# Recurrent states moved as 2 KB rows and turned by products with the identity, in a decoder layer on one Trainium2 core

## The chip, the cores and the metric

The kernel runs on one core of a Trainium2 chip. The core has a matrix engine (TensorE, PE in the profile; its weight loads are listed apart as PEld), a vector engine (DVE), a scalar engine (ACT), a general engine (GpSimd, POOL) and a queue engine (SyncE, SP) that here only issues transfers. Each engine works through its own instructions in program order and waits on semaphores. Sixteen DMA engines move the data between device memory and the on-chip memory (128 partitions). Products are written to PSUM, of which a bank holds 128 x 512 numbers. The metric is the device time of the whole program in microseconds (us), lower being better.

## What is computed

One layer of a decoder for 256 prompt tokens and for 8 sample sequences with 4 new tokens each. A layer has an input projection, an RWKV-7 group of 16 heads, a sparse attention group of 16 heads, an output projection and a mixer of experts. The change touches the RWKV group of the samples alone. Each sample has, for each head, a state S of 64 x 64 (value x key), which is read, carried over four steps and written back:

```python
def step(S, inp):
    r_t, d_t, k_t, v_t, kk_t, a_t = inp
    sk = jnp.einsum('bhvk,bhk->bhv', S, kk_t)
    S = (S * d_t[:, :, None, :] - sk[..., None] * (kk_t * a_t)[:, :, None, :]
         + v_t[..., None] * k_t[:, :, None, :])
    return S, jnp.einsum('bhvk,bhk->bhv', S, r_t)
```

For 8 samples and 16 heads that is 2 MB of states in and 2 MB out. In device memory a state's rows are its 64 values v, each with 64 keys k (256 bytes).

## The kernel before

The program runs in stages, one after the other, each with several streams of work woven together: input projections with the prompt's recurrence, then the sample attention, then the prompt attention with the output projection, then the mixer. The order within a stage is written by generators: `weave` always advances the stream that is furthest behind by its weight. A scheduler, which runs a timeline of its own when the program is built, then sets the order on every engine, so a change in one stream moves rows of the others on all engines.

The stage of interest weaves three streams: `late` (the attention of the samples), `sample_states` followed by `sample_steps` (their recurrence), and `outcomes` (the end of the prompt's recurrence). It runs from about 556 to 756 us.

The attention stream has 20 units. For each, POOL gathers selected rows or SP loads window rows into tiles `co` (L453, L899; 512 KB each, a ring of 14), PE turns the keys (L920), multiplies with the queries (L939, new keys L945), ACT and DVE do the softmax, PE turns the probabilities (L964, L968) and applies them (L983). A `co` tile is given back when L983 has read it, and the gather of a later unit waits for that. L535 to L575 are the compressed branch and L1007 turns a finished output. The next stage uses the memory of these tiles again for its first loads (L1667 onward: prompt rows, gate weights, output weights).

The recurrence stream:

- `sample_states` loads four states at a time into the tile `big` (`S0`), one buffer, with 4 transfers a sample (L1240). Eight samples make 32 transfers. For each sample PE turns the 16 heads with 4 transposes of 128 x 128 (L1244) and ACT copies the bank to `S0T` (L1245): key on the partition, two heads side by side in the halves of the partitions.
- `sample_steps` begins with the first products of all eight samples, 128 products of 64 x 64 by 8 columns (L1259) into one bank, then 16 small copies to `Ua` and `Ya` (L1265, L1266).
- The coefficients between the four tokens (L1284 to L1287), the four steps (L1295, L1296), and the new states (L1322 on POOL, L1324 on PE, L1326 and L1327 on DVE) follow.
- For each sample PE turns the new state back with 4 transposes (L1332), ACT copies it to `S1` (L1334, two buffers), and SP writes it with 4 transfers (L1337).
- At the end come the group norm of `Ya` (L1342 to L1350) and the sum into `BV` (L1353, L1356).

All banks of this stream have the tag `ss`, of which there are two. In the profile a digit at the end of a name is left out, so `S1` stands there as `S`, `x1` as `x`.

Of the kernel before, what the change touches and what calls it, by code (L numbers as in the profile page):

```python
# [18 lines left out]
P = 128  # L19
# [129 lines left out]
def hybrid_decode_step(ctx: ExitStack, tc: tile.TileContext, a, outs, dbg=None):  # L149
    nc = tc.nc  # L150
    ve, sc, pe, gp, sy = nc.vector, nc.scalar, nc.tensor, nc.gpsimd, nc.sync
    stop = dbg.get("stop", 99) if dbg is not None else 99
# [34 lines left out]
    def bank(tag="pb"):  # L187
        places = [(pool, nm, n) for _, div in psum for t_, pool, nm, n in div for _ in range(n) if t_ == tag]
        turn[tag] = k = (turn.get(tag, -1) + 1) % len(places)
        pool, nm, n = places[k]  # L190
        return pool.tile([P, 512], F32, name=tag, tag=nm, bufs=n)
# [60 lines left out]
    ident = C0("ident")  # L252
# [108 lines left out]
    for q in range(8):  # L361
        pb = bank(("p0", "p1")[q % 2])
        for t in range(2):
            for e in range(2):
                k = 2 * q + e
# [32 lines left out]
    hs = (slice(0, 64), slice(64, 128))  # L398
# [820 lines left out]
            yield from outcome(s, 1, "ss", sp([P, 8, 64], "Y2", bufs=2, tag="PR"))  # L1219


    S0T = sPQ = sD = sBC = sUV = None

    def sample_states(sp):

        nonlocal S0T, sPQ, sD, sBC, sUV
        S0T, sS = sp([P, 8, 8, 64], "S0T"), sp([P, 8, 232], "sS")
        sPQ = sS[:, :, 0:64].rearrange("p j (q t) -> p q j t", q=2)
        sD = sS[:, :, 64:104]
        sBC = sS[:, :, 104:168].rearrange("p j (y t) -> p j y t", y=2)  # L1230
        sUV = sS[:, :, 168:232].rearrange("p j (y t) -> p j y t", y=2)
        sy.dma_start(sS[:, :, :200], RS[:, :, :])
        srw = a["state_rwkv"][0].rearrange("b (j2 jp h) v k -> b jp h v j2 k", jp=2, h=2)
        for b in range(8):
            if b % 4 == 0:
                S0 = sp([P, 4, 4, P], "big", bufs=1)
                for b_ in range(4):
                    for jp in range(2):
                        for h in range(2):
                            sy.dma_start(S0[hs[jp], b_, :, 64 * h:64 * h + 64], srw[b + b_, jp, h])  # L1240
                yield 4 if b else 6
            pb = bank("ss")
            for j2 in range(4):
                pe.transpose(pb[:, 128 * j2:128 * j2 + 128], S0[:, b % 4, j2, :], ident)  # L1244
            sc.copy(S0T[:, b].rearrange("p j v -> p (j v)"), pb)  # L1245
            yield 0.5

    def sample_steps(sm):
        nrw = outs[10][0].rearrange("b (j2 jp h) v k -> b jp h v j2 k", jp=2, h=2)
        Ua, Ya, Vc = sm([P, 4, 8, 8], "Ua"), sm([P, 4, 8, 8], "Ya"), sm([P, 4, 8, 8], "Vc")  # L1250
        b_ = bank("ss")
        bk = [b_[:, :256], b_[:, 256:]]
        for ph in range(2):
            for jj in range(4):
                for b in range(8):
                    for h in range(2):
                        q = (ph + h) % 2
                        j = 4 * q + jj
                        pe.matmul(bk[q][hs[h], 64 * jj + 8 * b:64 * jj + 8 * b + 8], S0T[hs[h], b, j, :],  # L1259
                                  sPQ[hs[h], :, j, b::8], start=True, stop=True)  # L1260
                yield 1
        for q in range(2):
            v5 = bk[q][:, :256].rearrange("p (j b q t) -> p q t j b", j=4, b=8, q=2)
            for t in range(4):
                ve.tensor_copy(Ua[:, t, 4 * q:4 * q + 4, :], v5[:, 0, t])  # L1265
                sc.copy(Ya[:, t, 4 * q:4 * q + 4, :], v5[:, 1, t])  # L1266
        gp.tensor_copy(Vc.rearrange("p t j b -> p j t b"), sUV[:, :, 0, :].rearrange("p j (t b) -> p j t b", t=4))
        yield 1

# [11 lines left out]
        for q in range(4):  # L1281
# [3 lines left out]
            pb = bank("ss")  # L1285
# [25 lines left out]
        for src, dst in ((sUV, UVt), (sBC, BCt)):  # L1311
            for q in range(2):
                pb = bank("ss")
# [4 lines left out]
        for j in range(8):  # L1318
            pb = bank("ss")
# [8 lines left out]
            yield 2  # L1328
        for b in range(8):
            pb = bank("ss")  # L1330
            for j2 in range(4):
                pe.transpose(pb[:, 128 * j2:128 * j2 + 128], S0T[:, b, 2 * j2:2 * j2 + 2, :].rearrange("p a b -> p (a b)"), ident)  # L1332
            S1 = sm([P, 4, P], "S1", bufs=2, tag="S0")
            sc.copy(S1.rearrange("p j c -> p (j c)"), pb)  # L1334
            for jp in range(2):
                for h in range(2):
                    sy.dma_start(nrw[b, jp, h], S1[hs[jp], :, 64 * h:64 * h + 64])  # L1337
            yield 0.5

        Yf = Ya.rearrange("p t j b -> p (t j b)")  # L1340
        pb = bank("ss")
# [4 lines left out]
        pb = bank("ss")  # L1346
# [281 lines left out]
    sp = Pool("sp", "left")  # L1628
# [129 lines left out]
    for t in range(2):  # L1758
        for q in range(4):
            x_ = x1c(t, 512 * q, 512)  # L1760
            normed = ve.tensor_scalar(x_, x_, lrr[:, t:t + 1], lv[:, t:t + 1], op0=OP.mult, op1=OP.add)
            pb = bank("pa")
            for e in range(4):
                pe.transpose(pb[:, 128 * e:128 * e + 128], x1c(t, 512 * q + 128 * e, 128), ident)
            for e in range(4):
                k = 4 * q + e
# [35 lines left out]
    rp([P, UG], "rows", bufs=NRW)  # L1802
    S1 = dp([P, 8, 2 * P], "S1")
    dp([P, NDB, P], "ur", bufs=NUR)
# [4 lines left out]
    got, rows_, last_dot = [0, 0], {}, []  # L1809
# [36 lines left out]
    for h in range(9):  # L1846
        S, QP = [], {2 * h - 2 + c: q_ for c, q_ in enumerate(QN)} if h else {}
        QN = [kq([P, NPR], "QP", bufs=6) for c in range(2)]
        for c in (2 * h, 2 * h + 1):
            if c < 16:  # L1850
                pb = bank("pj")
# [7 lines left out]
        if h in (3, 8):  # L1859
            with tc.issue_after(wl_[12 if h < 8 else -1]):  # L1860
                t = h // 8
# [188 lines left out]
    pb = bank("pb")  # L2050
# [39 lines left out]
    for k in range(P):  # L2090
# [12 lines left out]
        for t in range(2):  # L2103
            for wi, xi in ((ah, vh), (ah, vl), (al, vh)):
                for q in range(3):
                    n_ = min(512, FD - 512 * q)
                    pe.matmul(acc[3 * t + q][:, :n_], wi[:, P * t:P * t + P], xi[:, 512 * q:512 * q + n_],  # L2107
                              start=(k == 0 and wi is ah and xi is vh), stop=(k == P - 1 and wi is al))
# [7 lines left out]
        if 66 <= k < 114 and k % 6 == 0:  # L2116
            with tc.issue_after(ld_.ins):
# [6 lines left out]
                else:  # L2124
                    t_, nm = ((g2_, "ln2_g"), (b2_, "ln2_b"))[n_ // 2 - 2]
# [67 lines left out]
```

## Time and profile before

| what | value |
|---|---|
| runs, median (lowest to highest of 3) | 2453.99 us (2433.44 to 2458.53) |
| the profiled execution, its own time | 2450.29 us |
| its span, first to last instruction | 2448.5 us |
| mean granted clock of PE | 0.951 |
| state loads L1240: transfers, KB each | 32, 64 |
| state writes L1337: transfers, KB each | 32, 64 |

In the rows of the profile a group is line, engine, operation and `output<-inputs`, with the count behind an x. In a timeline a row stands for a run of equal instructions: start and length in us, and in brackets the idle time of the engine ahead of it with what ended it. The length includes the end of the last instruction, which overlaps the next row's start. The granted clock is the share of full speed that PE's clock had in that window.

### The profile page before, as it was taken

The page shows a single profiled execution, that of the slowest core. Times are in us where ns is not written, and L with a number is a line of the kernel's source. Part 1 is how long each engine was busy: PE and PEld are TensorE (multiplying, and loading weights), DVE is VectorE, ACT ScalarE, POOL GpSimd, SP SyncE. Part 2 cuts the span into 40 slices and gives each one's busy share as a digit, 9 for nine tenths or more (in the row PEclk, how much of TensorE's full clock was granted, in tenths as well). Part 3 has the DMA queues.
Part 4 walks back from the last instruction along what each step waited for, and adds up shares of the span by engine and source line. Part 5 has one row for each costly group of instructions (what it writes and reads, how often), then busy time and mean ns, then how long its engine had stood idle before and what let it go on. Part 6 is the DMA issues. An engine that isn't in the chain of part 4 may idle for free.

```text
span 2448.5 us, 42558 instructions
## 1 busy us (share of the span) xinstructions
PE 2255.8 (92%) x15628; PEld 1888.4 (77%) x15628; DVE 1762.0 (72%) x4049; ACT 823.4 (34%) x1601; POOL 1332.6 (54%) x1347
## 2 busy tenths in 40 slices
PE   7988999897988998679999999999999899999996
PEld 7877889894645565558888888887777788887885
DVE  4788766555563355687877777556777899998888
ACT  4433222223432334221111111111777544444343
POOL 5687522324355011666766556565443688886772
PEclk9989999998896799789999999999999999999998
DMA  7777885448578784979999999999664799999994
GB/s 219 215 232 233 257 236 172 131 135 250 200 248 250 249 274 172 317 253 348 317 367 377 391 371 387 345 395 345 186 188 142 284 362 360 358 367 356 345 360 183
DMA packets 327600, 684.07 MB, mean 279 GB/s; under 512 B 82270, under 2 KB 200992, under 8 KB 326464
## 3 DMA queue, kind: packets, MB, share of 16 engines
q1 hardware_dynamic: 246176, 342.58, 42.2%
q0 software_dynamic: 81216, 338.78, 38.6%
q8 instruction: 123, 2.02, 0.3%
q14 instruction: 85, 0.70, 0.1%
HBM read 665.69 MB, written 23.88 MB: 282 GB/s over the span
## 4 chain that ended last, share of the span: by engine, by line
PE 29%; DMA 9%; DVE 8%; issue 7%; POOL 4%; ACT 1%; POOLq 0%; DVEq 0%; SPq 0%; ACTq 0%
PE pb L2107 20%; DMA rows<-in_peer_u_g,gi 8%; POOL rows L453 4%; PE px L1945 3%; DVE rows L1825 2%; PE pa L1978 2%; PE pj L1855 2%; PE pt L1937 1%; PE fs L1997 1%; DVE sr L1586 1%; DVE vl L2100 1%; DMA wraw<-in_peer_wq 0%; ACT vh L2099 0%; PE pa L1690 0%; DVE cw L1586 0%
## 5 line engine op out<-in xcount | busy, mean ns | idle before, releaser
L1899 PE MATMUL ph<-Xfd,ur 128*128 128x256 f32 x2304 | 497.6, 379 | 0.0
L1899 PEld LDWEIGHTS ph<-Xfd,ur 128*128 128x128 f32 x2304 | 437.6, 190 | 59.4
L453 POOL DMA_INDIRECT rq<-in_peer_v_g,gi x256 | 382.2, 1493 | 145.8 <-DVE fP L2080 85.6
L453 POOL DMA_INDIRECT rows<-in_peer_u_g,gi x256 | 313.3, 1224 | 189.3 <-DVE rows L1825 119.0
L1825 DVE SCALAR_TENSOR_TENSOR rows<-rows,x1a 128x896 f32<-128x896 f32 x256 | 278.8, 1097 | 136.2 <-DMA rows<-in_peer_u_g,gi 135.5
L422 PE MATMUL pj<-XH,wl 128*128 128x288 f32 (+1 forms) x752 | 233.5, 311 | 15.8 <-DVE wl L417 9.1
L422 PE MATMUL pj<-XH,wh 128*128 128x288 f32 (+1 forms) x752 | 232.1, 309 | 14.6 <-DVE ss L752 6.0
L422 PE MATMUL pj<-XL,wh 128*128 128x288 f32 (+1 forms) x752 | 228.0, 303 | 0.0
L2080 DVE SCALAR_TENSOR_TENSOR fP<-rq,ge,fP 128x640 f32<-128x640 f32 x254 | 223.7, 881 | 2.5
L2107 PE MATMUL pb<-vl,ah 128*128 128x512 f32 (+1 forms) x768 | 205.9, 376 | 0.8
L2107 PE MATMUL pb<-vh,al 128*128 128x512 f32 (+1 forms) x768 | 205.0, 375 | 0.0
L1900 ACT COPY AW<-ph 128x256 f32<-128x256 f32 x128 | 76.6, 612 | 370.5 <-PE ph L1899 362.7
L2107 PE MATMUL pb<-vh,ah 128*128 128x512 f32 (+1 forms) x768 | 185.6, 376 | 13.4 <-ACT vh L2099 10.9
L415 ACT CAST wh<-wraw 128x512 fp32r<-128x512 f32 (+1 forms) x188 | 115.1, 616 | 240.3 <-PE pj L422 191.1
L2107 PEld LDWEIGHTS pb<-vh,ah 128*128 128x128 f32 x768 | 144.1, 194 | 35.5 <-ACT vh L2099 13.9
L422 PEld LDWEIGHTS pj<-XH,wl 128*128 128x128 f32 (+1 forms) x752 | 145.8, 194 | 26.8 <-DVE wl L417 12.4
L476 DVE SCALAR_TENSOR_TENSOR CA<-co,wbc,CA 128x256 f32<-128x256 f32 x248 | 131.5, 568 | 46.5 <-DMA co<-in_cache_cmp_kv,gidx 46.5
L422 PEld LDWEIGHTS pj<-XH,wh 128*128 128x128 f32 (+1 forms) x752 | 146.1, 194 | 21.0 <-ACT wh L415 6.7
L2107 PEld LDWEIGHTS pb<-vl,ah 128*128 128x128 f32 x768 | 144.1, 194 | 22.7 <-DVE vl L2100 3.8
L2107 PEld LDWEIGHTS pb<-vh,al 128*128 128x128 f32 x768 | 144.5, 194 | 19.3
L422 PEld LDWEIGHTS pj<-XL,wh 128*128 128x128 f32 (+1 forms) x752 | 146.4, 195 | 1.5 <-issue 1.2
L417 DVE TENSOR_TENSOR wl<-wraw,wh 128x512 fp32r<-128x512 f32 (+1 forms) x141 | 100.8, 722 | 49.0 <-ACT wh L415 48.7
(871 smaller groups left out, 4335.6 us busy)
## 6 DMA issues: line engine op xcount, KB each, us to landing
ur<-in_peer_u_t SPq DMA_DIRECT2D x128, 576.0 KB
wraw<-in_w_in SPq DMA_DIRECT2D x152, 256.0 KB
cw<-in_w_out SPq DMA_DIRECT2D x32, 512.0 KB
wraw<-in_w_out SPq DMA_DIRECT2D x32, 512.0 KB
wraw<-in_peer_wq SPq DMA_DIRECT2D x32, 512.0 KB
cw<-in_peer_wq SPq DMA_DIRECT2D x32, 512.0 KB
wraw<-in_w_in SPq DMA_DIRECT2D x64, 128.0 KB
co<-in_state_win_kv SPq DMA_DIRECT2D x16, 512.0 KB
```

Source lines behind the costliest of these rows:

```text
L415: sc.copy(wh[:, :, :n], w[:, :, :n])
L417: i_ = en.tensor_tensor(wl[:, :, :n], w[:, :, :n], wh[:, :, :n].bitcast(F32), OP.subtract)
L422: last[2] = pe.matmul(pb[:n, :nt], wi[:, k, :n], xi[(o + k) // 8][:, (o + k) % 8, :nt], start=(o + k == 0 and wi is wh and xi is xh), stop ...
L453: gp.indirect_dma_start(out=dst, out_offset=None, in_=rows_, in_offset=bass.IndirectOffsetOnAxis(ap=ix, axis=0))
L476: ve.scalar_tensor_tensor(d_, x_, w_, d_, op0=OP.mult, op1=OP.add)
L1825: i_ = ve.scalar_tensor_tensor(r_, r_, 1.0, X1a[t], op0=OP.mult, op1=OP.mult, accum_out=h_)
L1855: pe.matmul(pb[:, :NPR], w[:, k, :], XT[:, o + k, :], start=(o + k == 0), stop=(o + k == 15))
L1899: mm = pe.matmul(ph[:, :NPR], w[:, e, :], Xfd[:, e, :], start=(e == 0), stop=(e == NDB - 1))
L1900: return mm, sc.copy(AW[:, i1 // 64, :, i1 % 64], ph[:, :NPR])
L1945: pin(pe.matmul(px[:, 128 * e:128 * e + 128].rearrange("p (c j) -> p c j", c=2), oT[:, e, :], AW[:, :, 4 * u + e, :], start=True, stop=True))
L2080: ve.scalar_tensor_tensor(fP[t], r_, w_, fP[t], op0=OP.mult, op1=OP.add)
L2107: pe.matmul(acc[3 * t + q][:, :n_], wi[:, P * t:P * t + P], xi[:, 512 * q:512 * q + n_], start=(k == 0 and wi is ah and xi is vh), stop=(k ...
```

## The change

Of a head's 64 rows eight follow one another on a partition now: partition 8j + o of a half holds rows 8o to 8o + 7 of head 2j + h, 512 numbers in one piece, 2 KB in device memory. A sample takes 2 transfers (one for each h) where it took 4. Since the rows of a head no longer lie on 64 partitions, the state is turned in 8 steps i, each for both halves, by a product of the 64 x 64 slice with the identity: 16 products a sample where 4 transposes were. The copy to `S0T` puts the columns back in the order of v. On the way out the same is done in reverse, with the products reading every eighth column of `S0T`. The first products of a sample (L1255 now) follow its turn, in a bank of their own, with one DVE and one ACT copy of 128 x 32; `Ua` and `Ya` are made in `sample_states`. From L1264 to L1323 line numbers are 3 lower than before, from L1340 on 2 lower.

```diff
+    def state_rows(st_, b, h):
+        return bass.AP(tensor=st_.tensor, offset=st_.offset + 65536 * b + 4096 * h, ap=[[8192, 8], [512, 8], [1, 512]])
...
-                S0 = sp([P, 4, 4, P], "big", bufs=1)
+                S0 = sp([P, 4, 8, 64], "big", bufs=1)
                 for b_ in range(4):
-                    for jp in range(2):
-                        for h in range(2):
-                            sy.dma_start(S0[hs[jp], b_, :, 64 * h:64 * h + 64], srw[b + b_, jp, h])
+                    for h in range(2):
+                        sy.dma_start(S0[hs[h], b_].rearrange("p i k -> p (i k)"), state_rows(a["state_rwkv"][0], b + b_, h))
...
-            for j2 in range(4):
-                pe.transpose(pb[:, 128 * j2:128 * j2 + 128], S0[:, b % 4, j2, :], ident)
-            sc.copy(S0T[:, b].rearrange("p j v -> p (j v)"), pb)
+            for i in range(8):
+                for h in range(2):
+                    pe.matmul(pb[hs[h], 64 * i:64 * i + 64], S0[hs[h], b % 4, i, :], ident[hs[h], hs[h]], start=True, stop=True)
+            sc.copy(S0T[:, b].rearrange("p j (o i) -> p j o i", i=8), pb.rearrange("p (i j o) -> p j o i", i=8, j=8))
             yield 0.5
+            pb = bank("ss")
+            for ph in range(2):
+                for jj in range(4):
+                    for h in range(2):
+                        j = 4 * ((ph + h) % 2) + jj
+                        pe.matmul(pb[hs[h], 8 * j:8 * j + 8], S0T[hs[h], b, j, :], sPQ[hs[h], :, j, b::8],
+                                  start=True, stop=True)
+            v4 = pb[:, :64].rearrange("p (j q t) -> p q t j", j=8, q=2)
+            ve.tensor_copy(UY[0][:, :, :, b], v4[:, 0])
+            sc.copy(UY[1][:, :, :, b], v4[:, 1])
+            yield 1
...
-            for j2 in range(4):
-                pe.transpose(pb[:, 128 * j2:128 * j2 + 128], S0T[:, b, 2 * j2:2 * j2 + 2, :].rearrange("p a b -> p (a b)"), ident)
-            S1 = sm([P, 4, P], "S1", bufs=2, tag="S0")
-            sc.copy(S1.rearrange("p j c -> p (j c)"), pb)
-            for jp in range(2):
+            rows_ = S0T[:, b].rearrange("p j (o i) -> p i (j o)", i=8)
+            for i in range(8):
                 for h in range(2):
-                    sy.dma_start(nrw[b, jp, h], S1[hs[jp], :, 64 * h:64 * h + 64])
+                    pe.matmul(pb[hs[h], 64 * i:64 * i + 64], rows_[hs[h], i], ident[hs[h], hs[h]], start=True, stop=True)
+            S1 = sm([P, 512], "S1", bufs=2, tag="S0")
+            sc.copy(S1, pb)
+            for h in range(2):
+                sy.dma_start(state_rows(outs[10][0], b, h), S1[hs[h]])
```

The removed block of first products in `sample_steps` (L1249 to L1266) is the same work with all samples in one bank.

How this moves the rows of PE at the fourth and fifth state, that is at the seam between the two loads of four. `CT` holds the identity. Before, from the fourth state's transposes to the fifth's:

```order
L1244 MATMUL ss<-CT_61,big 128x128 x4
L1209 MATMUL ss<-CT_61,YT_106 128x128 x4
L552 MATMUL sa<-im,CT_141 128x32
...
L939 MATMUL sc<-kt,Qb 32x512 x4
L964 MATMUL st<-CT_61,S 128x128 x4
L968 MATMUL sa<-CT_61,S 32x128
L920 MATMUL sa<-CT_61,co 128x128 x2
L983 MATMUL sao<-co,pt 32x128 x15
L1244 MATMUL ss<-CT_61,big 128x128 x4
```

The same place now, in PE's rows, from the last of the fourth state's products to the fifth's:

```order
L1247 MATMUL ss<-CT_61,big 64x64 x2
L964 MATMUL st<-CT_61,S 128x128 x4
L920 MATMUL sa<-CT_61,co 128x128 x4
L575 MATMUL sao<-CA,PzT 32x128 x4
L920 MATMUL sa<-CT_61,co 128x128 x8
L1255 MATMUL ss<-sS,S0T 64x8 x16
L983 MATMUL sao<-co,pt 32x128 x16
L939 MATMUL sc<-kt,Qb 32x512 x4
L945 MATMUL st<-KN,Qb 32x32 x4
L920 MATMUL sa<-CT_61,co 128x128 x12
L1247 MATMUL ss<-CT_61,big 64x64 x14
```

One unit of attention (the lower L939 to L983 of the first piece) stood between the two states and now follows the fifth; the first products of the fourth state are there instead.

The first products in PE's rows before, after the last state had been turned, in one block with attention rows between:

```order
L1259 MATMUL ss<-sS,S0T 64x8 x14
L983 MATMUL sao<-co,pt 32x128 x8
L920 MATMUL sa<-CT_61,co 128x128 x3
L1259 MATMUL ss<-sS,S0T 64x8 x50
L920 MATMUL sa<-CT_61,co 128x128 x10
L1259 MATMUL ss<-sS,S0T 64x8 x16
```

And now, at the third state, PE's rows from the last of its turn on:

```order
L1247 MATMUL ss<-CT_61,big 64x64 x3
L939 MATMUL sc<-kt,Qb 32x512 x2
L1255 MATMUL ss<-sS,S0T 64x8 x16
L1247 MATMUL ss<-CT_61,big 64x64 x13
L552 MATMUL sa<-im,CT_141 128x32
```

The 128 products of the block have gone to eight places, 16 behind each state.

SP's rows at the end of the stage before, where `out<-S` writes a state and `co` is the last window load of the attention:

```order
L1337 DMA out<-S_9338 64x4x64 x4
L1337 DMA out<-S_9361 64x4x64
L899 DMA co<-in_state_win_kv 128x1024 x2
L1337 DMA out<-S_9361 64x4x64 x2
L899 DMA co<-in_state_win_kv 128x1024 x2
```

And SP's rows now, from the first write on:

```order
L1335 DMA out<-S_9437 8x8x512 x2
L1335 DMA out<-S_9470 8x8x512 x2
L1335 DMA out<-S_9517 8x8x512 x2
L1335 DMA out<-S_9545 8x8x512
L899 DMA co<-in_state_win_kv 128x1024 x2
L1335 DMA out<-S_9545 8x8x512
L899 DMA co<-in_state_win_kv 128x1024 x2
```

The last window loads stood behind the first sample's writes and now stand behind three and a half samples'. On PE the recurrence as a whole has moved one attention unit forward: the last state is turned back ahead of the 19th unit's last products (L983) where it was ahead of the 20th's.

More of the change, by code (lines that the diff above doesn't have):

```diff
@@ L1219, in outcomes @@
             yield from outcome(s, 1, "ss", sp([P, 8, 64], "Y2", bufs=2, tag="PR"))
-    S0T = sPQ = sD = sBC = sUV = None
+    S0T = sPQ = sD = sBC = sUV = UY = None
+    def state_rows(st_, b, h):
+        return bass.AP(tensor=st_.tensor, offset=st_.offset + 65536 * b + 4096 * h, ap=[[8192, 8], [512, 8], [1, 512]])
     def sample_states(sp):
-        nonlocal S0T, sPQ, sD, sBC, sUV
+        nonlocal S0T, sPQ, sD, sBC, sUV, UY
         S0T, sS = sp([P, 8, 8, 64], "S0T"), sp([P, 8, 232], "sS")
+        UY = [sp([P, 4, 8, 8], nm) for nm in ("Ua", "Ya")]
         sPQ = sS[:, :, 0:64].rearrange("p j (q t) -> p q j t", q=2)
@@ L1232, in sample_states @@
         sy.dma_start(sS[:, :, :200], RS[:, :, :])
-        srw = a["state_rwkv"][0].rearrange("b (j2 jp h) v k -> b jp h v j2 k", jp=2, h=2)
         for b in range(8):
             if b % 4 == 0:
-                S0 = sp([P, 4, 4, P], "big", bufs=1)
+                S0 = sp([P, 4, 8, 64], "big", bufs=1)
                 for b_ in range(4):
-                    for jp in range(2):
-                        for h in range(2):
-                            sy.dma_start(S0[hs[jp], b_, :, 64 * h:64 * h + 64], srw[b + b_, jp, h])
+                    for h in range(2):
+                        sy.dma_start(S0[hs[h], b_].rearrange("p i k -> p (i k)"), state_rows(a["state_rwkv"][0], b + b_, h))
@@ L1246, in sample_states @@
             yield 0.5
-    def sample_steps(sm):
[L1249 to L1266, printed above, removed]
+            pb = bank("ss")
@@ L1267, in sample_steps @@
+            yield 1
+    def sample_steps(sm):
+        (Ua, Ya), Vc = UY, sm([P, 4, 8, 8], "Vc")
         gp.tensor_copy(Vc.rearrange("p t j b -> p j t b"), sUV[:, :, 0, :].rearrange("p j (t b) -> p j t b", t=4))
```

## The prediction

> **What bounds the kernel now.** I read the page first, then the granted clock by stretches of time, then who waited for whom, then the two queues that the change touches.
>
> ```profile
> span 2448.5 us, 42558 instructions
> PE 2255.8 (92%) x15628; PEld 1888.4 (77%) x15628; DVE 1762.0 (72%) x4049; ACT 823.4 (34%) x1601; POOL 1332.6 (54%) x1347
> ...
> DMA packets 327600, 684.07 MB, mean 279 GB/s; under 512 B 82270, under 2 KB 200992, under 8 KB 326464
> ```
>
> TensorE (PE) is busy for 92% of the span, but that is a mean. The change works only in the stage of the sample attention, about 556 to 756 us. The windows of that stage (us, each engine's busy time with its instructions, granted clock, DMA share, GB/s) show what it is like:
>
> ```profile
> 556.00:756.00 200.00, 164.05 (x1826) 107.67 (x1825) 114.71 (x421) 78.98 (x196) 85.42 (x92) 0.89 0.70 225
> 552.00:556.00 4.00, 4.00 (x50) 3.52 (x49) 0.86 (x2) 0.95 (x2) 2.37 (x9) 1.00 0.28 61
> 560.00:580.00 20.00, 9.87 (x51) 7.04 (x51) 10.28 (x49) 4.13 (x10) 8.08 (x9) 0.62 1.03 320
> 572.00:576.00 4.00, 0.00 (x0) 0.00 (x0) 0.00 (x0) 0.00 (x0) 0.00 (x0) 0.50 1.07 356
> 580.00:584.00 4.00, 3.87 (x23) 2.61 (x22) 2.88 (x15) 1.92 (x4) 0.00 (x0) 0.77 0.22 50
> 612.00:616.00 4.00, 3.03 (x15) 2.99 (x16) 0.30 (x2) 1.32 (x3) 0.95 (x1) 0.57 1.05 341
> 616.00:620.00 4.00, 3.70 (x59) 2.06 (x58) 2.49 (x9) 1.27 (x3) 1.95 (x3) 1.00 0.86 215
> 620.00:624.00 4.00, 3.17 (x53) 2.54 (x53) 0.80 (x5) 1.95 (x5) 1.93 (x2) 0.85 0.91 313
> 624.00:628.00 4.00, 4.00 (x65) 3.54 (x61) 0.69 (x1) 0.00 (x0) 0.00 (x0) 0.50 0.46 185
> 636.00:640.00 4.00, 4.00 (x45) 2.72 (x38) 1.05 (x4) 0.85 (x3) 1.36 (x2) 0.50 0.82 265
> 640.00:644.00 4.00, 4.00 (x31) 3.58 (x29) 1.38 (x2) 1.17 (x2) 0.00 (x0) 0.59 0.67 261
> 644.00:648.00 4.00, 4.00 (x96) 3.13 (x94) 0.58 (x4) 1.41 (x4) 1.20 (x2) 1.00 0.21 54
> ```
>
> PE is busy for 164 of 200 us here, no other engine for more than 115, and DMA is at 0.70. So PE's in-order queue carries the stage, with 36 us of waiting in it, and a clock of 0.50 in some stretches: 572 to 576 (all engines idle, DMA full) and 624 to 640 (PE never idle, yet at half clock; the shares before and after, 0.85 and 0.59, put its ends at about 623 and 643). The waits of PE in the stage, and in its queue the rows that bear on the change:
>
> ```profile
> PE ss L1244 <- DMA big<-in_state_rwkv: 10.5, 2, 8.2
> PE sa L920 <- DMA co<-in_cache_sel_kv,sidx: 8.2, 11, 3.2
> ...
> 577.18 1.09 PE L1244 MATMUL ss<-CT,big 128*128 128x128 f32 x4 [8.23 <-DMA big<-in_state_rwkv]
> 612.97 1.08 PE L1244 MATMUL ss<-CT,big 128*128 128x128 f32 x4 [2.25 <-DMA big<-in_state_rwkv]
> 624.97 5.51 PE L1259 MATMUL ss<-sS,S0T 64*64 64x8 f32 x100
> 646.15 1.10 PE L1259 MATMUL ss<-sS,S0T 64*64 64x8 f32 x32
> 724.80 1.04 PE L1332 MATMUL ss<-CT,S0T 128*128 128x128 f32 x8
> 755.63 0.30 PE L1007 MATMUL st<-CT,od 128*128 128x128 f32 x1 [1.83 <-DVE od L1005]
> ```
>
> Two waits for state loads, 8.23 and 2.25 us, are the largest single cause. A hundred first products take 5.51 us at clock 0.50, about 54 ns from start to start; 32 of them take 1.10 us at clock 1.00, about 27 ns without the last one's tail of some 0.25.
>
> At the end of the stage SyncE's queue decides (the first row gives min, median and max ns of one issue, and first and last start; the others start, us, and the issue with its count):
>
> ```profile
> L1337 SPq DMA_DIRECT2D out<-S x32: 595/616/1747, 723.7 to 757.5; - x32
> ...
> 732.30 25.81 SPq L1337 DMA_DIRECT2D out<-S  x25
> 758.21 2.00 SPq L1667 DMA_DIRECT2D x<-in_x_prompt  x4
> ...
> 761.09 0.62 DVE L1356 TENSOR_TENSOR BV<-Ya,BV 128x64 f32<-128x64 f32 x4
> ```
>
> The last attention transpose starts at 755.63, but the next stage's first loads stand behind 25 state writes that run to 758.1, and the recurrent outputs are ready only at 761.7.
>
> **The change, part by part.**
>
> *Packets.* In 560 to 580 the DMA queues, with the packets, MB and share of 16 engines of each, were:
>
> ```profile
> q0 software_dynamic: 1307, 4.74, 64.5%
> q1 hardware_dynamic: 4523, 1.63, 37.7%
> ```
>
> Share times 16 engines times 20 us gives 206 engine-us for 1307 packets of queue 0 (gathers, 3.6 KB on average): 158 ns each, 23 GB/s an engine. Queue 1, mostly state rows of 256 B, gives 121 engine-us for 4523 packets: 27 ns each. A batch of four states (1 MB) is 4096 packets before: 4096 x 27 / 16 = 6.9 us of all engines. After, 512 packets of 2 KB, at the gathers' rate 89 ns each: 2.9 us. A batch costs 4 us less of a resource whose share is 1.03 from 560 to 580. PE need not get all of it, since the gathers share the engines and are unchanged. First wait: 8.2 becomes 5, a gain of 3 (ends: 8 and a loss of 2, if the batch lands later, below). Second wait: the order now has 9 rows of PE between the fourth state's products and the fifth's where it had 19, so PE asks sooner by about what the load lands sooner: gain 0 (ends +2, -2). The gathers' own waits, 8.2 us in eleven pieces, the longest (3.2 us) among the writes: gain 1 (ends 0, 3).
>
> The Trainium skill ("DMA: Bandwidth & Descriptors", on why a DMA increments its semaphore by 16) says that a copy is spread over the largest count up to 16 that divides the slowest dimension of both sides. The new pattern has 8 there, so by it a state copy would use 8 of the 16 engines; no row of before shows one. It is taken up as a rival.
>
> *Transposes become products.* Each state has 4 transposes less and 16 products of 64x64 more, each of them two PE instructions (as L1136 below, whose 8 products in the code are 16 in the trace). Sixteen states moved (eight in, eight out): 512 new instructions, 64 gone. What the removed one costs: 8 in 1.04 us, less a tail of 0.27, 0.11 us each, 0.44 a state. For the new ones, two rows of 64x64 at full clock:
>
> ```profile
> 541.59 1.14 PE L1136 MATMUL p<-rB,SC 64*64 64x64 f32 x16
> 548.98 0.68 PE L1159 MATMUL p<-Us,rB 64*64 64x64 f32 x16
> ```
>
> Without the tail of 0.22 that is 61 ns from start to start when successive products use the same rows, and 31 ns when they change halves. The new ones change both halves at every product, as L1159 is nearest to: 32 x 31 ns = 1.0 us a state, net 0.55, times 16 = 9 us (upper end, at 61 ns: 1.51 net, 24 us). Those on the write side fill gaps of a PE that waits for gathers there; I let 2 us of the 9 lie in these and charge 7 (ends 2 and 24).
>
> *First products batch by batch.* As many as before (256 instructions), with as many small copies: DVE and ACT each had 8 of 128x32, and have 8 again, at nothing: they lie beside PE's rows, and without that cover each would stand on the way with 0.2 us (the second row of the next fence). What changes is where the products stand: 16 behind each state instead of 256 in one block. The block is the stretch at clock 0.50 from 623 to 643. Its 13 us of products would be 7 at 27 ns; the attention rows between them lose about 5 in the same way. [...] Upper end 11, lower 0; I take 8, since the first drop, at 623, came after a pause and another pause can cause one again.
>
> What transposes do to the clock, the rows behind the second wait show: nothing else ran from 612.97 to 616.3.
>
> ```profile
> 613.85 1.06 PE L964 MATMUL st<-CT,S 128*128 128x128 f32 x4
> 614.71 0.42 PE L920 MATMUL sa<-CT,co 128*128 128x128 f32 x1
> 614.92 0.42 PE L968 MATMUL sa<-CT,S 128*32 128x128 f32 x1
> 615.13 1.25 PE L920 MATMUL sa<-CT,co 128*128 128x128 f32 x6
> 616.31 1.08 PE L983 MATMUL sao<-co,pt 128*32 128x128 f32 x32
> ```
>
> The clock was 0.57 in that window and 1.00 in the next, so transposes alone brought it up. The Trainium skill ("TensorE: Matmul & The Clock Gate", Part 4 on the PE-mode transpose) says that they don't count as busy for the gate; the trace disagrees. What it would give is the last rival.
>
> *New wait.* A state's products now need the copy just issued (S0T, 128x512, ACT). The rows of the old copy, of the small copies, and of a rearranging copy elsewhere:
>
> ```profile
> L1245 ACT COPY S0T<-ss x8: 564/586/592, 578.3 to 622.3; 128x512 f32<-128x512 f32 x8
> L1265 DVE COPY Ua<-ss x8: 174/182/192, 647.3 to 655.5; 128x32 f32<-128x32 f32 x8
> ...
> L1979 ACT COPY AW<-pa x64: 586/586/587, 1718.3 to 1915.6; 128x512 f32<-128x512 f32 x64
> ```
>
> The first and last take 0.59 us, so the new rearrangement is put at 0.59 too (ends 0.59 and 1.2). The order has attention rows ahead of most of these products; where it has only two score products (the third state) about 0.6 us is uncovered, and behind it stand the attention rows, whose tiles POOL and SP wait for. Charge 1 (ends 0 and 8 x 0.6 = 5).
>
> *The end.* Half as many write issues, 16, each seen at 0.6 us (32 of them took 33.8 with their waits). The recurrence moves one attention unit forward in PE's order and the last two units have nothing of it between them. The writes should then be through before attention, and the next loads wait for attention's last rows at about 753 instead of 758.2: gain 4 (ends 0 and 8; more than 8 would need attention itself to end sooner).
>
> **Sum**, against the profiled run's own 2450.29 us (span 2448.5): -3 (first wait) -0 -1 (gathers) -8 (clock) -4 (end) +7 (products) +1 (copy) = -8: **2442 us**. The median of the three runs shown is 2453.99, 3.7 above the profiled run, and they lie 25 apart.
>
> **Rivals.**
>
> *The loads don't come sooner.* State copies on 8 engines would take 512 x 89 / 8 = 5.7 us of those engines for a batch, against 6.9 of all sixteen, and these 8 also carry half the gathers. For it: the gathers are 4.74 of the 6.4 MB in 560 to 580 and unchanged. Against it: 256 packets an engine become 64. Then waits are 8 and 4 (gain 3 turns into a loss of 2), the gathers gain nothing, the end 2: 2442 + 5 + 1 + 2 = **2450**. Chance 0.20.
>
> *The new products are dearer and hold the clock low* (the other side). If small products run at 0.50, 512 x 54 ns = 28 us, less the 7 for the transposes, 21 instead of 7, and the gain of 8 is gone: 2442 + 14 + 8 = **2464**. It decides from about 45 ns an instruction (16 us and half of the clock's gain lost: no gain is left). For it: 624 to 640, at full busy and 0.50. Against it: the 64x64 stretches before 556 ran at 1.00. Chance 0.15.
>
> *All covers hold.* First wait 8, second 2, clock 11, end 8, gathers 3, products 7, copy 1: -24, **2426**; also if the next stage, at clock 0.50 from 756 to 804 (row below), starts in another state. Chance 0.13.
>
> ```profile
> 756.00:804.00 48.00, 42.73 (x161) 25.52 (x163) 15.99 (x44) 5.04 (x11) 27.40 (x54) 0.50 0.87 280
> ```
>
> *Products hold the clock where transposes don't.* Then the half-clock time behind the two waits goes as well: 0.77 over 4 us and 0.57 over 4 us are 1.8 and 3.4 us at 0.50, with the 2.8 us from 577.2 to 580 together 8, of which half is saved: 2442 - 4 = **2438**. The rule named above is this; the transposes at 613 speak against it. Chance 0.05.
>
> **How the numbers follow.** The forecast has 0.47, its own range 2433 to 2451, for the ends of one or two terms. The two outer rivals hold 0.15 and 0.13; the range leaves out a little of both, 2422 to 2465. A measurement of this kernel can tell about 1%, 24.5 us, from no change. Faster by that: nearly all of the third rival, and a little of the forecast where before is taken at its median, 0.16. Slower: a third of the second rival, with small pieces of the others, 0.06. Within 1%: 0.78.
>
> **What would show it.** The packet line loses about 14,000 of its packets under 512 B (2 x 8192 before). PE's wait for the state loads is 5 and 2 us; the first rival shows 8 or more. No stretch of more than 5 us at clock 0.50 between 620 and 645, or this term is wrong. L1247 and L1331 start every 31 ns; at 60 the second rival is on. SP's first load of the prompt rows stands no more than 2 us behind attention's last product. Wrong altogether would be a result outside the range with these five as said: then the time moved in a later stage, whose order the scheduler also wrote anew.

## The result, and the profile after

In twelve runs of each kernel the changed one took 2464.8 us at the median (2457.9 to 2482.1), the kernel before 2452.0 (2433.4 to 2463.3). The ratio is 1.0065, with a 95% interval of 1.0037 to 1.0093: slower by 0.65%, some 16 us. The forecast was 2442, its range 2422 to 2465. Two later measurements, beside other kernels, gave 1.0017 (0.9987 to 1.0047, so not clear of no change) and 1.0072 (1.0044 to 1.0100). All ratios are of fast executions alone and are not the quotients of the medians.

The changed kernel's page has the packets that were meant to go gone, and more TensorE instructions:

```profile
span 2458.1 us, 43384 instructions
PE 2272.1 (92%) x16076; PEld 1899.1 (77%) x16076; DVE 1763.6 (72%) x4049; ACT 825.2 (34%) x1601; POOL 1304.4 (53%) x1347
...
DMA packets 312499, 684.13 MB, mean 278 GB/s; under 512 B 65118, under 2 KB 183840, under 8 KB 311360
```

There are 17,152 packets under 512 B less, and the profiled execution took 2460.02 us, 9.7 more than that of before. To see where, I cut out the stage of the sample attention in each trace: from the start of L1184's last write, which precedes the load of the states' steps, to the start of attention's last transpose (L1007). First the kernel before, then the changed one (from and to, length, then busy time of PE, PEld, DVE, ACT, POOL, then granted clock, DMA share, GB/s):

```profile
556.20:755.60 199.40, 163.48 (x1821) 107.12 (x1819) 114.35 (x420) 78.98 (x196) 84.96 (x91) 0.89 0.71 226
```

```profile
549.10:768.50 219.40, 189.80 (x2270) 123.45 (x2268) 119.19 (x437) 79.99 (x196) 82.27 (x88) 0.91 0.64 219
```

The stage is 20 us longer. TensorE is busy 26 us longer in it and waits 6 us less; the granted clock is no lower and DMA is less used. (The 20 us show as 13 at the stage's end and 9.7 at the kernel's because before's execution came to the stage 7 us later, through rows that are the same in both.) Over 19 profiles, of before, the changed kernel and the experiments below, the last transpose starts between 747 and 798 us and the program ends 1679 to 1707 us later; the two times go together with a correlation of 0.85. So this stage decides most of it, but a single profile is a coarse measure: in two more profiles of the changed kernel the stage is 209.6 us (after_again) and 223.7 us (y_after).

The changed kernel's groups of TensorE instructions in the stage (busy us, mean ns | idle before them):

```profile
L1331 PE MATMUL ss<-CT,S0T 64*64 64x64 f32 x256 | 20.9, 289 | 0.0
L1247 PE MATMUL ss<-CT,big 64*64 64x64 f32 x256 | 17.5, 243 | 7.6 <-issue 7.5
...
L1255 PE MATMUL ss<-sS,S0T 64*64 64x8 f32 x256 | 10.2, 201 | 0.0
```

Instructions of neighbouring groups overlap at their edges. A share-out without overlap comes from the rows of the timeline: each line is charged with the time from its row's start to the next row's, less what the next one waited. Waits are those over 0.15 us, with the one before the last transpose.

| TensorE's time in the stage, us | before | after | difference |
|---|---|---|---|
| turns of the states that come in (L1244 / L1247) | 5.2 | 16.0 | +10.8 |
| turns of the states that leave (L1332 / L1331) | 4.6 | 19.6 | +15.0 |
| first products (L1259 / L1255) | 12.6 | 8.6 | -4.0 |
| attention's rows (with L1209 of `outcomes`) | 120.7 | 123.7 | +3.0 |
| the recurrence's other products | 20.3 | 21.9 | +1.6 |
| waits | 35.7 | 29.3 | -6.4 |

The turns alone are 25.8 us more. Three rows of the timeline show them in unbroken stretches at clock 1.00, each with the row that follows:

```profile
582.27 1.02 PE L1247 MATMUL ss<-CT,big 64*64 64x64 f32 x26
583.22 1.08 PE L983 MATMUL sao<-co,pt 128*32 128x128 f32 x32
...
737.47 1.66 PE L1331 MATMUL ss<-CT,S0T 64*64 64x64 f32 x24
739.06 1.08 PE L983 MATMUL sao<-co,pt 128*32 128x128 f32 x32
740.08 1.18 PE L1331 MATMUL ss<-CT,S0T 64*64 64x64 f32 x16
741.19 0.66 PE L964 MATMUL st<-CT,S 128*128 128x128 f32 x4
```

The 26 read products take the 0.95 us to the next row's start, 37 ns each; 24 write products take 1.59 us, 66 ns each, and 16 take 1.11 us, 69 ns. Between the first and the last start within these rows it is 32 ns for the read products and 60 ns for the write products; the rest falls at the row's ends. Both do the same arithmetic; the lines' own views (min, median, max ns) show where they differ:

```profile
L1247 PEld LDWEIGHTS ss<-CT,big x256: 129/135/228, 559.1 to 637.0; 64*64 64x64 f32 x128
L1247 PE MATMUL ss<-CT,big x256: 213/218/367, 559.1 to 637.1; 64*64 64x64 f32 x128
...
L1331 PEld LDWEIGHTS ss<-CT,S0T x256: 191/213/218, 715.2 to 755.9; 64*64 64x64 f32 x128
L1331 PE MATMUL ss<-CT,S0T x256: 280/281/333, 715.2 to 756.0; 64*64 64x64 f32 x128
```

The write products' weights lie eight elements apart, and loading them takes 213 ns instead of 135.

### The profile page after: what moved, and what is told of

Its sections match the earlier page's. It is cut to its first block, busy times and chain, and to the rows that moved or that the text cites. A ratio compares the mean times of both kernels' runs of the same rounds, so it can differ in the third digit from the quotient of the medians.

```text
span 2458.1 us, 43384 instructions
## 1 busy us (share of the span) xinstructions
PE 2272.1 (92%) x16076; PEld 1899.1 (77%) x16076; DVE 1763.6 (72%) x4049; ACT 825.2 (34%) x1601; POOL 1304.4 (53%) x1347
## 4 chain that ended last, share of the span: by engine, by line
PE 51%; DVE 3%; issue 2%; ACT 1%; DMA 1%; POOL 0%; DVEq 0%; POOLq 0%; SPq 0%; ACTq 0%
PE ph L1897 20%; PE pb L2105 18%; PE pj L1853 4%; PE px L1943 3%; PE pa L1976 2%; PE pt L1935 2%; PE fs L1995 1%; ACT vh L2097 1%; DMA wraw<-in_peer_wq 1%; DVE vl L2098 1%; DVE cw L1584 0%; PE pb L1372 0%; DVE AW L2151 0%; DVE oo L1931 0%; POOL cw L453 0%
## 5 line engine op out<-in xcount | busy, mean ns | idle before, releaser
L453 POOL DMA_INDIRECT rows<-in_peer_u_g,gi x256 | 292.7, 1143 | 208.5 <-DVE rows L1823 135.5
L2078 DVE SCALAR_TENSOR_TENSOR fP<-rq,ge,fP 128x640 f32<-128x640 f32 x254 | 223.7, 881 | 2.5
L2105 PE MATMUL pb<-vh,ah 128*128 128x512 f32 (+1 forms) x768 | 186.7, 378 | 13.4 <-ACT vh L2097 10.9
L2105 PEld LDWEIGHTS pb<-vh,al 128*128 128x128 f32 x768 | 145.0, 194 | 19.5
```

Source lines behind the costliest of these rows:

```text
L453: gp.indirect_dma_start(out=dst, out_offset=None, in_=rows_, in_offset=bass.IndirectOffsetOnAxis(ap=ix, axis=0))
L2078: ve.scalar_tensor_tensor(fP[t], r_, w_, fP[t], op0=OP.mult, op1=OP.add)
```

## The experiments

All ratios are to the kernel before, run in the same call on the same chip, with 95% intervals. "In" and "out" are TensorE's time in the turns of the states that come and leave, "waits" its waits, in us, in the stage of the run's one profile, reckoned as above (e3_contig is the kernel of y_contig, whose profile stands for both).

| kernel | median, before's median | ratio (interval) | in | out | waits |
|---|---|---|---|---|---|
| e1_read | 2457.0, 2454.7 | 0.9995 (0.9967-1.0023) | 16.0 | 4.1 | 35.2 |
| e2_write | 2465.9, 2454.7 | 1.0015 (0.9985-1.0045) | 5.1 | 17.8 | 42.0 |
| e3_contig | 2475.2, 2454.7 | 1.0073 (1.0046-1.0101) | | | |
| e4_batch | 2471.9, 2454.7 | 1.0060 (1.0029-1.0091) | 6.1 | 5.0 | 45.2 |
| x_block | 2474.2, 2450.7 | 1.0080 (1.0050-1.0110) | 13.3 | 17.9 | 33.6 |
| x_double | 2492.2, 2450.7 | 1.0176 (1.0133-1.0218) | 15.9 | 36.4 | 33.5 |
| p1_both | 2449.2, 2450.7 | 1.0008 (0.9979-1.0037) | 11.7 | 3.8 | 29.6 |
| p1_block | 2448.3, 2450.7 | 0.9995 (0.9968-1.0022) | 11.0 | 3.8 | 32.6 |
| after_again | 2447.1, 2440.4 | 1.0017 (0.9987-1.0047) | 13.3 | 19.5 | 23.1 |
| h_write | 2437.9, 2440.4 | 0.9993 (0.9962-1.0024) | 12.4 | 9.4 | 26.2 |
| x_dread | 2459.8, 2440.4 | 1.0077 (1.0053-1.0100) | 21.4 | 17.9 | 25.7 |
| n_order | 2445.4, 2440.4 | 1.0016 (0.9989-1.0043) | 5.5 | 4.7 | 38.2 |
| y_after | 2467.6, 2449.2 | 1.0072 (1.0044-1.0100) | 16.0 | 20.3 | 28.5 |
| y_write | 2463.5, 2449.2 | 1.0051 (1.0021-1.0081) | 4.9 | 17.9 | 38.3 |
| y_contig | 2468.4, 2449.2 | 1.0065 (1.0036-1.0093) | 17.1 | 13.4 | 33.4 |
| y_batch | 2465.9, 2449.2 | 1.0058 (1.0028-1.0089) | 6.1 | 5.4 | 43.3 |
| z_batch_late | 2462.7, 2450.4 | 1.0044 (1.0015-1.0073) | 5.3 | 4.7 | 36.7 |
| q_early | 2456.9, 2450.4 | 1.0026 (1.0003-1.0050) | 5.4 | 4.8 | 42.4 |

**One side at a time.** e1_read has the changed kernel's read side and before's write side, e2_write the reverse; y_write is e2_write again.

```diff
 e1_read, against the changed kernel
-            rows_ = S0T[:, b].rearrange("p j (o i) -> p i (j o)", i=8)
-            for i in range(8):
-                for h in range(2):
-                    pe.matmul(pb[hs[h], 64 * i:64 * i + 64], rows_[hs[h], i], ident[hs[h], hs[h]], start=True, stop=True)
+            for j2 in range(4):
+                pe.transpose(pb[:, 128 * j2:128 * j2 + 128], S0T[:, b, 2 * j2:2 * j2 + 2, :].rearrange("p a b -> p (a b)"), ident)
...
+            for jp in range(2):
+                for h in range(2):
+                    sy.dma_start(nrw[b, jp, h], S1[hs[jp], :, 64 * h:64 * h + 64])
```

> The changed kernel's read side alone (2 KB packets in, identity products, first products batch by batch), with the 128x128 transposes and the 64 KB writes of before on the write side. Theory A (the loss is the write products, which start every 62 ns in the changed kernel's trace where the read products start every 31): 2440 to 2453 us, 12 to 20 us under the changed kernel, and L983's last instruction back before 760. Rival B (the loss is the read side or the products batch by batch): 2458 to 2467, as the changed kernel. If both sides lose alike: about 2458.

> The changed kernel's write side alone (identity products from strided rows, 2 KB packets out); reads, transposes in and the block of first products as before. Theory A: 2460 to 2468 us, that is all of the loss (256 instructions at 62 ns, 16 us, in place of 32 transposes in about 4). Rival B: 2448 to 2454. If both sides lose alike: about 2458.

> The write side of the change alone, once more beside the changed kernel. Theory D (the write products' TensorE time is the loss): within 5 us of the changed kernel, 6 to 15 us over before. If the loss needs the read side or the batches too: within 3 us of before.

The read side alone costs nothing that can be measured; its interval ends at 0.23%, 6 us. In its profile 11 us more of turns stand against 4 us less of first products, the waits as a whole are as long as before's, and the stage is 208.8 us, 9 longer; why the kernel's time doesn't show that stays open. The write side alone was unclear at first and is slower by 0.21 to 0.81% in the second measurement, where the changed kernel itself is slower by 0.44 to 1.00%. That is the side that theory A named. Its reason, the strided weights, is what the next pair asked for.

**The strided weights.** In e3_contig, and in y_contig again, the write products take adjacent columns, so the states leave in another order:

```diff
-                    pe.matmul(pb[hs[h], 64 * i:64 * i + 64], rows_[hs[h], i], ident[hs[h], hs[h]], start=True, stop=True)
+                    pe.matmul(pb[hs[h], 64 * i:64 * i + 64], S0T[hs[h], b, i, :], ident[hs[h], hs[h]], start=True, stop=True)
```

> The changed kernel, but the write products take 64 adjacent columns (the state of head i) as their weights where it takes every eighth column; the states that leave are therefore in another order, and nothing else differs in number or size. Theory A (the strided weights double the product): the write products start every 31 ns, about 8 us of TensorE time go, and the kernel takes 2454 to 2460. Rival: they still start every 62 ns (another reason, such as the clock), and the time stays at 2460 to 2468.

> The changed kernel with adjacent columns as weights of the write products (the states leave in another order), once more beside the changed kernel on one chip. By TensorE's time (13.5 instead of 19.6 us in the profiles): 4 to 8 us under the changed kernel. If the strided weights' time is covered: within 3 us of it or above.

The write products of y_contig, in their line's view:

```profile
L1330 PEld LDWEIGHTS ss<-CT,S0T x256: 129/135/228, 716.5 to 753.6; 64*64 64x64 f32 x128
L1330 PE MATMUL ss<-CT,S0T x256: 212/218/366, 716.5 to 753.6; 64*64 64x64 f32 x128
```

The weights load in 135 ns again, and in rows of 16 and more a product takes 34 to 43 ns, the row's ends included. So the stride is what makes one such product dear. TensorE's time out falls by 6.9 us against y_after, but 4.9 us come back as waits and 1.1 in the read turns, and the kernel is no faster (1.0065 beside 1.0072). The intervals still leave room for several us; whether the stride costs the kernel anything is open. With adjacent columns 13.4 us remain, 8.8 more than before's transposes.

**Doubling and halving.** x_double issues each write product twice, x_dread each read product; h_write leaves half of the write products out.

```diff
 h_write
-            for i in range(8):
+            for i in range(4):
...
-            sc.copy(S1, pb)
+            sc.copy(S1.rearrange("p (a c) -> p a c", a=2), pb[:, None, :256].to_broadcast([P, 2, 256]))
```

> The changed kernel with each write product issued twice into the same place (256 more TensorE instructions, 14 to 20 us of its time, behind which the same states leave). If TensorE's time in this stretch is paid in full: 2478 to 2488. If it is hidden beside the attention's waits and the loss has another cause: 2462 to 2472.

> The changed kernel with half of the write products: only the first four of eight row sets of each state are turned, and the copy takes these twice, so half of the rows that leave hold other rows' values; copy, packets and everything else keep their size. Theory D (TensorE's time on the write side is paid in full: doubling it added 17 us of its time and about 27 to the kernel): TensorE's time there falls from 20 to about 10 us and the kernel to 2450 to 2458. If the loss sits elsewhere (read side, batches, packets): 2460 to 2470.

> The changed kernel with each read product issued twice into the same place (256 more TensorE instructions at 37 to 60 ns, 10 to 16 us). Theory D says that the read side is partly covered, since the read side alone cost nothing measurable (0.9995): 2464 to 2472, clearly less than the 27 us that doubling the write products added. If TensorE's time is paid wherever it falls in this stage: 2478 to 2492.

> The changed kernel once more, as the yardstick on this chip for the two kernels beside it, and for a second execution to be read. 2458 to 2472 us, 10 to 18 over the kernel before.

x_double's stage, in the same columns as above:

```profile
551.50:798.40 246.90, 213.24 (x2526) 145.23 (x2525) 120.71 (x437) 80.59 (x196) 81.47 (x88) 0.88 0.58 194
```

17 us more of write products make the stage 27 us longer than the changed kernel's (37 and 23 against its other two profiles), and the ratio goes from 1.0065 (1.0072 and 1.0017 in other calls) to 1.0176: paid in full, and more. Leaving out half of the write products, 10 us of TensorE's time, took the ratio from 1.0017 to 0.9993: the expected direction, but the intervals overlap, the more so as after_again itself lost less than the 10 to 18 us expected. Doubled read products, 8 us more of turns, cost 0.6 points, resolved beside after_again: this side isn't free either, which theory D had put lower. In e1_read, which gains on the first products, no such price showed.

**The same packets with cheaper turns.** p1_both keeps 2 KB packets on both sides, but fills the 128 partitions with the rows of two samples. Then 128 read instructions do for 256, and on the write side a transpose of 128x128 again does both heads at once. p1_block is the same with the first products in one block, x_block the changed kernel with that block alone.

```diff
 p1_both
+                    for h in range(2):
+                        sy.dma_start(S0[:, b_, h].rearrange("p i k -> p (i k)"), state_rows(a["state_rwkv"][0], b + 2 * b_, h))
...
+                    for h in range(2):
+                        pe.matmul(pb[hs[h], 128 * (i % 4):128 * (i % 4) + 128], S0[:, b % 4 // 2, h, i, :], ident, start=True, stop=True)
...
+            rows_ = S0T[:, b:b + 2].rearrange("p b j (o i) -> p i (b j o)", i=8)
...
+                pe.transpose(pb[:, 128 * (i % 4):128 * (i % 4) + 128], rows_[:, i], ident)
```

> The changed kernel with the first products in one block behind all eight states, as before; packets of 2 KB and identity products on both sides stay. Theory C (the two causes are TensorE's time in the identity products, 16 us in and 20 us out against 5 and 5 for the transposes, and, on its own, the batch-by-batch order, which cost 15 us alone): 2452 to 2462 us, that is some of the loss gone. If only the products count: 2462 to 2470, as the changed kernel. If only the batches count: 2450 to 2456.

> 2 KB packets on both sides as in the changed kernel, but two samples side by side: the rows of a pair of samples fill the 128 partitions, with both heads behind one another in the free dimension. Read side 64 identity products over 128 partitions (128 instructions instead of 256), write side 32 transposes of 128x128 instead of 256 instructions; 8 loads and 8 writes of 256 KB. First products batch by batch. If TensorE's time in the products is the loss: 2445 to 2456. If the batches are the loss: 2460 to 2470.

> As the kernel with pairs of samples, but with the first products in one block as before. Theory C: 2440 to 2452, no slower than before and the lowest of these. If the packets themselves (2 KB, fewer and longer transfers) are the loss: 2460 or more.

x_block, without the batches, is at 1.0080 no faster than the changed kernel in its three measurements, so in this kernel the batches are not the loss. x_block and p1_block differ only in the pairing of samples: half as many transfers of twice the size, one buffer S1 of double size instead of two, and the cheaper turns. The stage and the two groups of turns, of x_block:

```profile
546.70:774.00 227.30, 193.30 (x2266) 128.82 (x2265) 116.95 (x437) 80.35 (x196) 82.39 (x87) 0.86 0.62 210
...
L1335 PE MATMUL ss<-CT,S0T 64*64 64x64 f32 x256 | 18.6, 292 | 0.0
L1246 PE MATMUL ss<-CT,big 64*64 64x64 f32 x256 | 14.6, 239 | 5.9 <-DMA big<-in_state_rwkv 5.9
```

and of p1_block:

```profile
551.90:757.60 205.70, 172.74 (x1913) 110.89 (x1914) 115.98 (x424) 82.27 (x196) 82.22 (x88) 0.89 0.67 230
...
L1248 PE MATMUL ss<-CT,big 128*64 128x128 f32 x128 | 11.9, 305 | 4.4 <-DMA big<-in_state_rwkv 4.4
L1340 PE MATMUL ss<-CT,S0T 128*128 128x128 f32 x32 | 4.3, 278 | 0.0
```

The turns are 17 us less (18.6 + 14.6 against 4.3 + 11.9), the stage 22, and 1.0080 becomes 0.9995. Nearly all of the 22 us is TensorE's busy time (193.30 against 172.74; what the turns leave of it goes with the clock, 0.86 against 0.89), and the waits differ by 1 us, so an effect of the larger transfers doesn't show. In the same call p1_both stands at 1.0008, so with cheap turns no difference between batches and a block can be measured. With the doubling this shows the cause: the turns' TensorE time, on both sides, the greater part on the write side. It also bounds what the packets are worth: 17,000 packets fewer and turns that are still 5 us dearer than before's (14.8 against 9.8) make together no difference that can be measured. No kernel here is measurably faster than the one before.

**Batches alone.** The kernel before with only the first products moved behind each state (e4_batch, y_batch) is slower, twice, with hardly more TensorE time in the turns. z_batch_late keeps that work and shifts the place of the sample stream among the attention by one share of the weaving; n_order and q_early keep before's work and shift only its place.

```diff
 z_batch_late, against e4_batch
-            yield 1
+            yield 2
 q_early, against before
-            yield 0.5
+            yield 0.1
...
-                yield 1
+                yield 0.5
```

> The kernel before with one part of the change: the first products batch by batch, each behind its state's copy, with one small copy on VectorE and one on ScalarE a batch. Packets, transposes and writes as before. Theory A: 2446 to 2456 us, no difference. Rival B (waits of TensorE behind the copies, or the new order of the attention rows, cost the time): 2458 or more.

> The products batch by batch alone, once more. If its 15 us were a property of the kernel: 10 to 20 us over before. If they were that chip's or chance: within 5 us of before.

> The kernel before with no work changed: the shares by which the weaving of the streams places the states' turns and the block of first products are shifted (1.5 instead of 0.5 behind each state, nearly nothing behind the pieces of the block), so that the same instructions stand among other attention rows. It asks how much the place alone is worth, since the products batch by batch alone cost 15 us with hardly more TensorE time. If place matters little: 2446 to 2458. If it is worth as much as that run lost: 2462 or more, or 2442 or less.

> The products batch by batch alone, as the kernel that lost 14 to 15 us twice, with one share of the weaving raised (2 instead of 1 behind each batch), so that the sample stream stands later among the attention: its new-state products behind tiles 178 to 256 of the attention's 320 turns (136 to 220 in the kernel that lost, 193 to 273 in the kernel before), its group norm behind the last one as before (291 there). Theory E (its loss is the place: the sample stream ran ahead and left the attention's waits uncovered, each followed by about 10 us at a granted clock of 0.50): 2446 to 2456 by a kernel before at 2450, within 5 us of before. If the batches themselves cost: 10 to 20 us over before.

> The kernel before with its work unchanged and its sample stream moved ahead by two shares of the weaving (0.1 instead of 0.5 behind each state, 0.5 instead of 1 behind the pieces of the block of first products): new-state products behind tiles 148 to 228, group norm at 291. Theory E: 8 to 18 us over before, by place alone. If place is worth little: within 5 us of before.

What the loss looks like in one profile is seen in 5 us windows and in the waits of TensorE from 640 to 710, first of before:

```profile
645.00:650.00 5.00, 5.00 (x85) 2.73 (x84) 2.15 (x16) 2.45 (x10) 1.90 (x2) 1.00 0.56 197
690.00:695.00 5.00, 4.14 (x29) 2.50 (x29) 3.68 (x8) 1.18 (x4) 3.89 (x4) 1.00 0.99 387
695.00:700.00 5.00, 4.48 (x59) 2.50 (x60) 3.39 (x13) 1.44 (x3) 2.48 (x3) 1.00 0.72 255
...
PE sa L552 <- DVE im L549: 0.3, 1, 0.3
```

and of y_batch:

```profile
645.00:650.00 5.00, 2.35 (x28) 1.70 (x17) 4.15 (x24) 2.41 (x7) 1.66 (x3) 1.00 0.97 367
690.00:695.00 5.00, 2.02 (x16) 0.80 (x8) 4.40 (x6) 1.86 (x6) 4.51 (x5) 0.94 0.94 342
695.00:700.00 5.00, 4.61 (x14) 2.67 (x15) 2.73 (x15) 0.75 (x3) 0.05 (x1) 0.50 0.78 318
700.00:705.00 5.00, 5.00 (x22) 2.34 (x21) 1.73 (x3) 0.59 (x1) 0.00 (x0) 0.50 0.00 0
...
PE sa L552 <- DVE im L549: 4.0, 2, 3.4
```

TensorE stands before a product of the compressed branch (L552) that waits 3.4 us for DVE, and then works at clock 0.50. That the sample stream had run ahead is theory E's reading. But the place is at most part of it: moved back, the waits (36.7 us) and the stage (201 us) are near before's again and the batches still cost 0.15 to 0.73%, and q_early, with the place alone, costs 0.03 to 0.50%, in its middle 6 us where theory E asked for 8 to 18. n_order's smaller shift can't be told from nothing. The rest of the batches' loss stays open; in kernels with 2 KB reads (e1_read, p1_both) the batches show none.

## Why the prediction failed

The change was put within 1% with 0.78, and it is; but a gain was forecast and a loss measured. Two terms of the sum failed, the products by their size and the end of the stage by its sign.

**The products: the term that failed.** It read +7, from 512 instructions at 31 ns, less the transposes, less 2 us that were to lie in waits. Measured are +10.8 and +15.0. Three things were missing. The 31 ns hold inside an unbroken row of read products (32 above), but the row's ends were taken off as a tail: with them it is 37 ns. The write side was priced like the read side, though the code shows that its weights come from every eighth column: 66 to 69 ns. And rows that the scheduler breaks up cost more each: the 256 read products stand in 26 pieces among attention rows and take 62 ns on average, low clock included; the write products take 77. The upper end, 24 us at 61 ns, was about right by luck: it was the price of products that share their rows. How much of the products lay in gaps isn't shown: TensorE's waits fell by 6.4 us in all, and the next terms' waits are in that.

**The end of the stage: the wrong sign.** A gain of 4 was to come when the writes are through before attention. SyncE's rows after are:

```profile
750.64 7.60 SPq L1335 DMA_DIRECT2D out<-S  x4
758.34 2.66 SPq L1665 DMA_DIRECT2D x<-in_x_prompt  x4
```

Half as many writes end no sooner, since each waits for its write products, and the last of these starts at 756.0 where the last transpose started at 748.9. Attention's last transpose, from 755.6, moved to 768.5: the write products stand in front of its last units in TensorE's order. The promised sign, a prompt-row load at most 2 us behind attention's last product, came out with the load ahead of it; it could not tell a faster queue from a slower attention.

**Where it was right.** First wait, -3: right in size, not in kind. The waits of 8.2 and 2.25 us for the loads are gone, and 7.5 us in 13 pieces stand among the read products, the longest 1.4, together 3.0 less. The profile calls them "issue", which is time in which it shows nothing to wait for; most lie where DMA is at 0.95 and more, and what they wait for stays open. In after_again it is 4.1 us, put down to the loads. Gathers, -1: it was -6.0 (8.2 to 2.2) here and -2.1 in after_again, perhaps because the busier TensorE asks later. New wait, +1: the copy kept its 0.586 us, and one wait of 0.9 us for a small copy (L1283 behind Ya) is what shows. Low clock, -8: the stretch at 0.50 from 623 to 643 did go, and the first products fell from 12.6 to 8.6 us. The rest of that gain was given back in new stretches, as the text had feared for "another pause":

```profile
596.00:600.00 4.00, 2.18 (x36) 1.73 (x35) 1.28 (x6) 1.32 (x3) 2.32 (x3) 0.96 0.99 277
600.00:604.00 4.00, 3.83 (x20) 2.46 (x24) 2.03 (x8) 1.99 (x5) 0.00 (x0) 0.50 0.98 303
612.00:616.00 4.00, 2.65 (x18) 1.82 (x17) 0.85 (x5) 0.42 (x2) 0.94 (x1) 0.67 0.95 368
616.00:620.00 4.00, 4.00 (x18) 1.84 (x17) 1.17 (x3) 1.11 (x3) 0.00 (x0) 0.50 0.10 40
```

What keeps the clock up, on which this term rests, is shown by no run. Wide rows alone don't bring it back at once: in y_batch it stayed at 0.50 for 10 us and more behind the 3.4 us wait, though the rows there have 128 and 512 columns (L920, L1320).

**The rivals.** The second, products dearer, came to 2464, and 2464.8 was measured, with the products above its limit of 45 ns an instruction. That the two numbers meet is luck, and so is it that the result lies inside the range, whose upper part stands for this rival. Its reason was only half right: the products were dear at clock 1.00 too, for their weights and their broken rows, the stage's mean clock rose from 0.89 to 0.91, and half of the clock's gain came. It had 0.15, and with one row of 16 instructions as the price it deserved more. The first rival (copies on half of the DMA engines) was not tried by itself; p1_both's pattern has 16 in place of 8, and no gain from that can be told apart there.

## What to carry to other kernels

Where TensorE's in-order queue carries a stage, price a layout change by its instructions first: here 448 more of them cost more than 17,152 packets fewer returned. Look at the stride of the operand that is loaded as weights, and at how often the scheduler will break the rows up, before taking a start-to-start time from one clean stretch. If a layout needs more turns, put two samples or heads side by side until a 128x128 transpose does the work again.

## What the runs showed of the hardware

- Weights of 64 columns that lie eight elements (32 B) apart load in 213 ns (median) against 135 for adjacent ones, and such products start 60 to 66 ns apart within a row of 16 or more against 30 to 34. For transposes of 128x128 with the same stride the load is dearer too, first p1_block's and then before's:

```profile
L1340 PEld LDWEIGHTS ss<-CT,S0T x32: 185/193/208, 724.0 to 746.2; 128*128 128x128 f32 x32
```

```profile
L1332 PEld LDWEIGHTS ss<-CT,S0T x32: 137/140/146, 718.2 to 748.8; 128*128 128x128 f32 x32
```

  Yet these turns as a whole took no longer (3.8 against 4.6 us).
- In y_batch TensorE stood idle for 3.4 us from 692.0. The mean of 0.94 over the 5 us from 690 puts the fall to 0.50 at about 694.4, 2.4 us into the pause, and the clock stood at 0.50 for the next 10 us although TensorE was busy for 4.61 and 5.00 us of each five. The Trainium skill ("TensorE: Matmul & The Clock Gate", Part 1) puts both the fall and the return at a window of about 3.4 us; here the fall came somewhat sooner and the return later.
- The kernel before had medians from 2440.4 to 2454.7 us in six measurements, and the changed kernel lost 0.65, 0.17 and 0.72% in three, so kernels of different calls can't be compared within some 10 us.
